# A PSUM bank for the wide Newton chains, and POOL for four groups' rotations, in a two-layer transformer kernel

## The chip, the cores and the metric

The kernel runs on one core of a Trainium2 chip. The metric is device microseconds from the start to the end of one execution; lower is better. Engines are named as in the profile: PE is the matrix engine and PEld its weight loads, DVE is VectorE, ACT is ScalarE, POOL is GpSimd, SP issues DMAs.

## The reference, cut to what matters

Two layers over x of 1024 tokens by 1024 channels. Layer 0 mixes with 12 heads of decayed causal attention, layer 1 with 12 heads of causal attention whose queries and keys come from low-rank latents; both add 4 heads of cross attention to a memory of 256 tokens. Each layer ends in a gated feed-forward with a short convolution. The change touches two things of it:

```python
def rmsnorm(x, g):
    xf = x.astype(jnp.float32)
    y = xf * lax.rsqrt(jnp.mean(xf * xf, axis=-1, keepdims=True) + EPS)
    return (y * g.astype(jnp.float32)).astype(x.dtype)

def rope(x, cos, sin):
    half = x.shape[-1] // 2
    x1, x2 = x[..., :half], x[..., half:]
    return jnp.concatenate([x1 * cos - x2 * sin, x1 * sin + x2 * cos], axis=-1)
```

Queries, keys and latents are normalised with `rmsnorm` per head; in layer 1 the last 32 of a query's 96 channels are rotated first.

## The kernel before, in words

Matmuls run in fp32r on values split in a high and a low part, so most products are three matmuls. The stages follow one another: normalisation and projection of layer 0 by six pairs of heads (`pair`, L1206), first attention (`attention`, L286), output projection (L679), feed-forward (`FFN`, L731), then projection of layer 1, second attention, output projection and feed-forward.

PSUM has three pools (L119 to L132): `psS`, two pairs of banks for scores; `psO`, one bank for attention outputs; `psX`, three banks for everything else: transposes, the chunks of the pass that finds each row's maximum, and projections. A tile takes a free buffer of its pool and gives it back after its last access.

`rsqrt` (L211) computes 1/sqrt(mean + EPS) on DVE with two setting-up instructions (L219 or L221, L222) and three Newton steps. With width 1 a step is two instructions (L228, L229). With a wider operand, 2 to 32 columns, it is three (L231 to L233). The wide form is called 21 times: six times by `pair`, twice in the memory's preparation, once for the first layer's memory queries (L1322, called before the first attention), and in layer 1 twice for its memory queries, four times by `latents` (L1590) and once by `scale_k` (L1543) of each of six groups.

A group (`Group`, L1489) is two heads of the second attention. Its pieces, in order: `begin` loads and splits the weights and sets a column of ones in the V tile (L1509); then twice: two `project`, `squares` (POOL squares, DVE sums) and `rotate`; at the end `scale_k` and `scale_q`, which multiply keys and queries by the result of `rsqrt`, on DVE and, for the rotated part of k, on POOL (L93). `rotate` calls `rope` (L1475): four multiplications and an addition and a subtraction on 128x128, two of the multiplications on POOL and the other four instructions on DVE, through a tile of the pool `tmp`, whose two buffers `squares` and the weight load share.

The order of work in the second attention: heads run one behind the other, four memory heads first. PE's order is the order of the program, since every matmul is pinned (L101 to L107, `pin`). Between the score and output units of a head, pieces of other work are put at fractions of the head's length (`TIMES`, L279; `spread`, L1674): the transposes that prepare the head after the next, the next head's maximum pass in ten chunks (matmul, then DVE, L299 or L304) and its `final` (a transpose and a DMA), and the pieces of the group two heads ahead. The order of the other engines is set by a planner at build time, from a simulated timeline (`schedule_with_timeline_sim`), by program order among what is ready in it. On POOL, the second attention also computes the low part of each block of probabilities (`plo`, L347), which the pinned output matmuls read.

The lines for the steps below: L211 to L234, L1475 to L1487, L1509, L1541, L125, L290 to L315, L522 to L526.

Of the kernel before, what the change touches and what calls it, by code (L numbers as in the profile page):

```python
# [7 lines left out]
F32 = mybir.dt.float32  # L8
# [4 lines left out]
OP = mybir.AluOpType  # L13
# [4 lines left out]
P = 128  # L18
D = 1024
S = 1024  # L20
NT = S // P
# [53 lines left out]
def hybrid_kernel(ctx: ExitStack, tc: tile.TileContext, A, out):  # L75
    nc = tc.nc
# [4 lines left out]
    def copy(eng, o, i):  # L81
        if eng == "a":
            nc.scalar.copy(o, i)  # L83
        elif eng == "v":
            nc.vector.tensor_copy(o, i)
        else:
            nc.gpsimd.tensor_copy(o, i)

    def sub(eng, o, a, b):
        (nc.vector if eng == "v" else nc.gpsimd).tensor_tensor(o, a, b, op=OP.subtract)  # L90

    def mul(eng, o, a, b):
        (nc.vector if eng == "v" else nc.gpsimd).tensor_tensor(o, a, b, op=OP.mult)  # L93

    def split(hi, lo, src, he="a", le="p"):
        copy(he, hi, src)
        sub(le, lo, src, hi.bitcast(F32))
# [27 lines left out]
    def psX():  # L125
        return psum.tile([P, 512], F32, name="psX", tag="X", bufs=3)
# [7 lines left out]
    def open_pool(name, bufs, **kw):  # L134
        return tc.alloc_tile_pool(name=name, bufs=bufs, reuse_waits="tile", **kw)

    const = open_pool("const", 1)
    small = open_pool("small", 2)
# [22 lines left out]
    ones1 = const.tile([P, 64], F32, name="ones1")  # L161
# [48 lines left out]

    def rsqrt(ss, n, width):  # L211

        v = small.tile([P, 32], F32, name="rs_v")[:, :width]
        y = small.tile([P, 32], F32, name="rs_y", bufs=6)[:, :width]
        t = small.tile([P, 32], F32, name="rs_t")[:, :width]
        if isinstance(n, tuple):
            w = width // len(n)
            for i, m in enumerate(n):
                nc.vector.tensor_scalar(v[:, i * w:(i + 1) * w], ss[:, i], 1.0 / m, EPS, op0=OP.mult, op1=OP.add)  # L219
        else:  # L220
            nc.vector.tensor_scalar(v, ss, 1.0 / n, EPS, op0=OP.mult, op1=OP.add)  # L221
        nc.vector.tensor_scalar(y.bitcast(I32), v.bitcast(I32), -0.5, 1597463007.0, op0=OP.mult, op1=OP.add)  # L222
        if width == 1:
            nc.vector.tensor_scalar(v, v, -0.5, None, op0=OP.mult)
        for i in range(3):
            if width == 1:

                nc.vector.tensor_scalar(t, y, y, v, op0=OP.mult, op1=OP.mult)  # L228
                nc.vector.tensor_scalar(y, t, 1.5, y, op0=OP.add, op1=OP.mult)  # L229
            else:  # L230
                nc.vector.tensor_tensor(t, y, y, op=OP.mult)  # L231
                nc.vector.scalar_tensor_tensor(t, t, -0.5, v, op0=OP.mult, op1=OP.mult)
                nc.vector.scalar_tensor_tensor(y, t, 1.5, y, op0=OP.add, op1=OP.mult)  # L233
        return y  # L234

# [4 lines left out]
    class Norm:  # L240
# [5 lines left out]
        def stats(self, *ts):  # L246
            ss = small.tile([P, 4], F32, name="n_ss", bufs=3)
            for i, t in enumerate(ts):
                sumsq(ss[:, i:i + 1], self.src(t), D)
            y = rsqrt(ss[:, :len(ts)], D, len(ts))  # L250
            for i, t in enumerate(ts):
                self.r[t] = y[:, i:i + 1]
# [953 lines left out]
    def pair(c, W, extra=()):  # L1206
# [4 lines left out]
        for t in range(NT):  # L1211
# [17 lines left out]
            for f in extra[:n]:  # L1229
                f()  # L1230
            del extra[:n]
        r = rsqrt(ss.rearrange("p t i -> p (t i)"), HD, 32).rearrange("p (t i) -> p t i", t=NT)
        for i, T in ((0, q), (2, k)):
            Tv = T.rearrange("p (t h d) -> p t h d", t=NT, h=2)
# [3 lines left out]
    class Memory:  # L1238
# [35 lines left out]
        def finish(self):  # L1274
            pb = [self.ps[:, t * 512:(t + 1) * 512] for t in range(2)]
            ss = small.tile([P, 2, NMH], F32, name="m_ss", bufs=1)
            for t in range(2):
                for h in range(NMH):
                    sumsq(ss[:, t, h:h + 1], pb[t][:, h * HD:(h + 1) * HD], HD)
            r = rsqrt(ss.rearrange("p t h -> p (t h)"), HD, 2 * NMH).rearrange("p (t h) -> p t h", t=2)  # L1280
            for t in range(2):
                nc.vector.tensor_tensor(kmem[:, t, :].rearrange("p (h d) -> p h d", h=NMH),
                                        pb[t][:, 0:MEM].rearrange("p (h d) -> p h d", h=NMH),
                                        r[:, t, :, None].to_broadcast([P, NMH, HD]), op=OP.mult)
                v = pb[t][:, MEM:512].rearrange("p (h d) -> p h d", h=NMH)
                copy("a", VHm[:, t, :, 0:64], v)
                sub("v", VLm[:, t], v, VHm[:, t, :, 0:64].bitcast(F32))
# [184 lines left out]
            nc.vector.tensor_scalar(r, r, 3.1415925, -3.1415925, op0=OP.min, op1=OP.max)  # L1472
            nc.scalar.activation(dst, r, AF.Sin)

    def rope(x, n, t0, nt):  # L1475

        x1, x2 = x[..., 0:16], x[..., 16:32]
        c = cos[:, t0:t0 + nt, None, :].to_broadcast([P, nt, n, 16])
        s = sin[:, t0:t0 + nt, None, :].to_broadcast([P, nt, n, 16])
        y = tmp.tile([P, 768], F32, name="rope", tag="t")[:, :4 * nt * n * 16].rearrange(  # L1480
            "p (j t n d) -> p j t n d", j=4, t=nt, n=n)
        mul("v", y[:, 0], x1, c)
        mul("p", y[:, 1], x2, s)
        mul("v", y[:, 2], x1, s)
        mul("p", y[:, 3], x2, c)
        sub("v", x1, y[:, 0], y[:, 1])
        nc.vector.tensor_tensor(x2, y[:, 2], y[:, 3], op=OP.add)  # L1487

    class Group:  # L1489

# [5 lines left out]
        def begin(self):  # L1496
            g = self.g
            raw = tmp.tile([P, 768], F32, name="g_raw", tag="t")[:, :640]
            nc.sync.dma_start(raw[:, 0:384].rearrange("p (c j) -> p c j", c=2),
                              wq[:, g * 192:(g + 1) * 192].rearrange("(c p) j -> p c j", p=P))  # L1500
            nc.sync.dma_start(raw[:, 384:640], wkv[:, g * 256:(g + 1) * 256])
            self.w = gw.tile([P, 2, 640], F32R, name="g_w")
            split(self.w[:, 0], self.w[:, 1], raw, "a", "p")
            gp, vp = gpools[g % 2], vpools[min(g % 3, 1)]
            self.q = gp.tile([P, NT, 2, QK], F32, name="gq")
            self.k = gp.tile([P, NT, 2, QK], F32, name="gk")
            self.vh = vp.tile([P, NT, 2, 65], F32R, name="g_vh")
            self.vl = vp.tile([P, NT, 2, 64], F32R, name="g_vl")
            nc.vector.tensor_copy(self.vh[:, :, :, 64], ones1[:, 0:16].rearrange("p (a b) -> p a b", a=NT))  # L1509
            self.ss = small.tile([P, 2, NT, 2], F32, name="g_ss", bufs=2)  # L1510

        def project(self, u):
# [25 lines left out]
                nc.vector.tensor_reduce(self.ss[:, j, ts], sq, axis=AX, op=OP.add)  # L1538

        def rotate(self, i):  # L1540
            rope(self.q[:, i * 4:i * 4 + 4, :, 64:96], 2, i * 4, 4)  # L1541

        def scale_k(self):  # L1543
            nc.vector.tensor_tensor(self.ss[:, 0], self.ss[:, 0], ss_kr[:, :, None].to_broadcast([P, NT, 2]), op=OP.add)
# [107 lines left out]
    def swap():  # L1652
        latent(7)
        latents(6)
        rope(kr[:, :, None, :], 1, 0, NT)
        for p in (w1, xtp, hp):
            p.release()
        pl.pf, pl.p, pl.nplo = open_pool("pf1", 2), open_pool("p1", 3), 3
        pl.pools = [open_pool("gB", 1), open_pool("vB", 2), open_pool("qkB", 1)]
        gpools.append(pl.pools[0])  # L1660
        vpools.append(pl.pools[1])
        qk_set(pl.pools[2], 1)
# [16 lines left out]
    for g in range(1, 6):  # L1679
        p = groups[g].pieces()  # L1680
# [35 lines left out]
    t0 = at[10] - 1  # L1716
    bg.setdefault(t0, []).append((0.0, turn_over))
    for j in range(6):
        i, x = divmod(t0 + 0.1 + 0.28 * j, 1.0)
# [48 lines left out]
```

## Time and profile before

| | us |
|---|---|
| median of 3 runs | 2527.79 (2522.3 to 2529.79) |
| the profiled execution | 2524.59 |
| its span, first to last instruction | 2522.8 |
| PE busy | 2369.9 (94%) |
| DVE busy | 1892.6 (75%) |
| ACT busy | 1209.5 (48%) |
| POOL busy | 985.3 (39%) |
| mean granted TensorE clock | 0.970 |

The span leaves 1.8 us of the execution outside. Busy times are unions of an engine's instructions. PE at 94% leaves some 150 us in which it waits; the views by window say where these lie.

### The profile page before, as it was taken

Reading aid. Unit: us, or ns where it says so; the run is one execution under the profiler, and the core shown is the slowest. Engines: PE = TensorE matmul, PEld = TensorE weight load, DVE = VectorE, ACT = ScalarE, POOL = GpSimd, SP = SyncE. Lnnn points to the kernel's source line nnn. Section 1 sums busy time; section 2 is a strip of 40 time slices with the busy share of each in tenths; the row PEclk is TensorE's granted clock in tenths of the full one; section 3 lists DMA queues with packets and bytes.
Section 4 is the critical chain, followed back from the end, with each engine's and each line's share of the span. In section 5 each row is a group of like instructions: output and inputs, shape, how many; then the busy total and the mean of one; then the engine's idle time right before and its main releaser. Section 6 shows DMA issues by size and latency. Waiting matters only on the chain.

```text
span 2522.8 us, 32481 instructions
## 1 busy us (share of the span) xinstructions
PE 2369.9 (94%) x11609; PEld 1954.7 (77%) x11609; DVE 1892.6 (75%) x3183; ACT 1209.5 (48%) x2341; POOL 985.3 (39%) x640
## 2 busy tenths in 40 slices
PE   7999899998999999989998798889979999998999
PEld 7999666677788888868888576767868888886887
DVE  7432677757778878789997868774488788778997
ACT  5544678723444444434454555555244444443443
POOL 1221467743233233234332566666132333233342
PEclk9999899999999999999999899989989999999999
DMA  4221121253132232451230101010512222226221
GB/s 143 84 51 27 35 61 47 52 177 109 51 92 76 84 92 76 161 190 52 99 134 11 34 23 27 19 38 22 192 56 84 87 81 84 83 85 242 84 101 67
DMA packets 163651, 208.89 MB, mean 83 GB/s; under 512 B 11175, under 2 KB 124682, under 8 KB 163490
## 3 DMA queue, kind: packets, MB, share of 16 engines
q1 hardware_dynamic: 162054, 206.63, 25.9%
q8 instruction: 92, 1.51, 0.2%
q14 instruction: 69, 0.57, 0.1%
q10 hardware_dynamic: 1436, 0.18, 0.0%
HBM read 153.34 MB, written 39.98 MB: 77 GB/s over the span
## 4 chain that ended last, share of the span: by engine, by line
PE 73%; DVE 17%; issue 3%; DMA 3%; POOL 2%; ACT 2%; SPq 0%; DVEq 0%; ACTq 0%; POOLq 0%
PE psX L102 32%; PE psS L102 25%; PE psO L102 14%; DVE f_op L90 2%; PE psX L106 2%; POOL f_op L90 1%; DVE mA L299 1%; DVE psX L304 1%; DVE f_x L1143 1%; DVE KB L525 1%; DVE f_T L90 1%; DMA rrow<-rec 1%; DVE f_d L90 1%; DVE QB L525 1%; DVE f_S L90 1%
## 5 line engine op out<-in xcount | busy, mean ns | idle before, releaser
L90 POOL TENSOR_TENSOR f_op<-f_S,f_op 128x512 fp32r<-128x512 f32 x184 | 272.0, 1479 | 671.0 <-ACT f_op L83 613.7
L102 PE MATMUL psS<-f_T,f_op 128*128 128x512 f32 x1584 | 382.4, 393 | 7.8 <-DVE f_T L90 5.9
L90 POOL TENSOR_TENSOR plo<-pf,ph 128x1024 fp32r<-128x1024 f32 (+2 forms) x160 | 315.1, 1980 | 158.0 <-ACT pf L343 95.7
L102 PEld LDWEIGHTS psS<-f_T,f_op 128*128 128x128 f32 x1584 | 297.0, 189 | 68.9 <-DVE f_T L90 6.5
L102 PE MATMUL psX<-f_B,f_op 128*128 128x512 f32 x1260 | 296.3, 389 | 0.1
L83 ACT CAST f_op<-f_S 128x512 fp32r<-128x512 f32 x248 | 153.6, 621 | 279.0 <-PE psS L102 109.2
L102 PEld LDWEIGHTS psX<-f_B,f_op 128*128 128x128 f32 x1260 | 236.4, 188 | 49.6 <-issue 0.5
L102 PE MATMUL psS<-f_op 128*128 128x512 f32 x960 | 222.4, 390 | 0.4 <-DVE f_op L90 0.4
L102 PEld LDWEIGHTS psS<-f_op 128*128 128x128 f32 x960 | 180.7, 188 | 39.0 <-DVE f_op L90 1.2
L102 PE MATMUL psX<-f_op 128*128 128x512 f32 x666 | 175.3, 403 | 20.8 <-DVE f_op L90 18.1
L102 PE MATMUL psX<-w_w,hTh 128*128 128x384 f32 (+2 forms) x672 | 167.8, 333 | 2.2 <-ACT hTh L83 2.2
L102 PEld LDWEIGHTS psX<-f_op 128*128 128x128 f32 x666 | 127.9, 194 | 54.0 <-DVE f_op L90 24.2
L898 DVE SCALAR_TENSOR_TENSOR f_v<-f_cv,cw,f_v 128x1023 f32<-128x1023 f32 x88 | 150.9, 1715 | 7.6 <-ACT f_v L896 6.2
L342 ACT ACTIVATE ph<-psS 128x1024 fp32r<-128x1024 f32 (+2 forms) x131 | 112.4, 858 | 90.4 <-PE psS L102 83.4
L83 ACT CAST f_op<-f_raw 128x512 fp32r<-128x512 f32 x148 | 91.4, 621 | 132.3 <-PE psS L102 67.1
L102 PE MATMUL psX<-KA,QA 66*128 66x128 f32 (+4 forms) x320 | 111.0, 395 | 24.5 <-DVE mA L299 10.5
L83 ACT CAST f_op<-f_d 128x512 fp32r<-128x512 f32 x144 | 84.3, 619 | 102.0 <-PE psS L102 35.6
L858 DVE TENSOR_TENSOR f_u<-psS,f_p 128x512 f32<-128x512 f32 x44 | 30.4, 691 | 126.7 <-PE psS L102 126.7
L102 PEld LDWEIGHTS psX<-w_w,hTh 128*128 128x128 f32 x672 | 120.8, 190 | 3.2 <-ACT hTh L83 2.8
L898 DVE SCALAR_TENSOR_TENSOR f_v<-f_cg,cw,f_v 128x1023 f32<-128x1023 f32 x88 | 112.6, 1279 | 11.2 <-ACT f_v L896 11.2
L90 POOL TENSOR_TENSOR f_op<-f_d,f_op 128x512 fp32r<-128x512 f32 x52 | 75.3, 1448 | 115.9 <-ACT f_op L83 115.9
L102 PE MATMUL psS<-QA,KA 67*128 67x512 f32 (+7 forms) x304 | 110.9, 366 | 7.8 <-DMA QA<-mrow 7.8
(379 smaller groups left out, 5698.8 us busy)
## 6 DMA issues: line engine op xcount, KB each, us to landing
f_raw<-in_ffn_w_up_dram SPq DMA_DIRECT2D x88, 512.0 KB
g<-f_v SPq DMA_DIRECT2D x44, 512.0 KB
f_d<-g SPq DMA_DIRECT2D x36, 512.0 KB
f_d<-in_ffn_w_down_dram SPq DMA_DIRECT2D x36, 512.0 KB
w_raw<-in_fox_w_in_dram SPq DMA_DIRECT2D x48, 192.0 KB
rrow<-rec SPq DMA_DIRECT2D x32, 256.0 KB
wo_raw<-in_w_out_dram SPq DMA_DIRECT2D x32, 256.0 KB
xr<-x SPq DMA_DIRECT2D x16, 512.0 KB
```

What stands on the lines that cost most here:

```text
L83: nc.scalar.copy(o, i)
L90: (nc.vector if eng == "v" else nc.gpsimd).tensor_tensor(o, a, b, op=OP.subtract)
L102: r = nc.tensor.matmul(*a, **k)
L106: r = nc.tensor.transpose(*a, **k)
L299: nc.vector.tensor_reduce(mA[:, q0:q0 + n], px[:, :n * width].rearrange("p (a b) -> p a b", a=n), axis=AX, op=OP.max)
L304: nc.vector.tensor_tensor_reduce(px[:, off:off + nk], px[:, off:off + nk], mQ[:, 512 - nk:], scale=1.0, scalar=m if on else NEG, op0=OP.ad ...
L342: nc.scalar.activation(ph, ps[:, :w], AF.Exp)
L525: nc.vector.scalar_tensor_tensor(Tl[tl0:tl1, hs], px, gcol, Th[0:n, hs].bitcast(F32), op0=OP.mult, op1=OP.subtract)
L858: nc.vector.tensor_tensor(o, x, y, op=OP.add)
L898: nc.vector.scalar_tensor_tensor(v[:, k:], src[:, :S - k], cw[:, 2 - k, ch:ch + 1], v[:, k:], op0=OP.mult, op1=OP.add)
L1143: nc.vector.tensor_tensor(X[t][:, hs], X[t][:, hs], self.sets[st][v], op=OP.add)
```

## The change

In `rsqrt`, calls wider than one column keep the value `v` and the temporary `t` in one tile of `psX` instead of two small SBUF tiles; the result `y` stays in SBUF. The products are regrouped so that every instruction of a step has one operand in PSUM and at most one in SBUF: t = v*y, t = -0.5*t*y, y = (t+1.5)*y. Calls of width one keep SBUF tiles, now one column wide. In the second attention, groups 2 to 5 rotate wholly on POOL and set their columns of ones there; groups 0 and 1 and the rotation of the shared key part stay as they were.

```diff
     def rsqrt(ss, n, width):
 
-        v = small.tile([P, 32], F32, name="rs_v")[:, :width]
         y = small.tile([P, 32], F32, name="rs_y", bufs=6)[:, :width]
-        t = small.tile([P, 32], F32, name="rs_t")[:, :width]
+        if width == 1:
+            v = small.tile([P, 1], F32, name="rs_v")
+            t = small.tile([P, 1], F32, name="rs_t")
+        else:
+
+            px = psX()
+            v, t = px[:, 0:width], px[:, 32:32 + width]
...
-                nc.vector.tensor_tensor(t, y, y, op=OP.mult)
-                nc.vector.scalar_tensor_tensor(t, t, -0.5, v, op0=OP.mult, op1=OP.mult)
+                nc.vector.tensor_tensor(t, v, y, op=OP.mult)
+                nc.vector.scalar_tensor_tensor(t, t, -0.5, y, op0=OP.mult, op1=OP.mult)
                 nc.vector.scalar_tensor_tensor(y, t, 1.5, y, op0=OP.add, op1=OP.mult)
...
-    def rope(x, n, t0, nt):
+    def rope(x, n, t0, nt, eng="v"):
...
-        mul("v", y[:, 0], x1, c)
+        mul(eng, y[:, 0], x1, c)
         mul("p", y[:, 1], x2, s)
-        mul("v", y[:, 2], x1, s)
+        mul(eng, y[:, 2], x1, s)
         mul("p", y[:, 3], x2, c)
-        sub("v", x1, y[:, 0], y[:, 1])
-        nc.vector.tensor_tensor(x2, y[:, 2], y[:, 3], op=OP.add)
+        sub(eng, x1, y[:, 0], y[:, 1])
+        (nc.vector if eng == "v" else nc.gpsimd).tensor_tensor(x2, y[:, 2], y[:, 3], op=OP.add)
...
-            nc.vector.tensor_copy(self.vh[:, :, :, 64], ones1[:, 0:16].rearrange("p (a b) -> p a b", a=NT))
+            copy("p" if self.g > 1 else "v", self.vh[:, :, :, 64], ones1[:, 0:16].rearrange("p (a b) -> p a b", a=NT))
...
-            rope(self.q[:, i * 4:i * 4 + 4, :, 64:96], 2, i * 4, 4)
+            rope(self.q[:, i * 4:i * 4 + 4, :, 64:96], 2, i * 4, 4, "p" if self.g > 1 else "v")
```

## Rows read from the trace of the kernel before

**Rows 1.** Windows: stretch; busy us of PE, PEld, DVE, ACT, POOL; granted clock; DMA.

```profile
110.00:270.00 160.00, 158.83 (x994) 158.00 (x992) 56.05 (x200) 74.27 (x407) 35.41 (x27) 1.00 0.15 37
...
1395.00:1460.00 65.00, 49.34 (x242) 37.77 (x243) 56.05 (x111) 31.68 (x51) 35.46 (x24) 0.82 0.14 34
...
1500.00:1532.00 32.00, 26.54 (x152) 19.59 (x151) 30.07 (x56) 17.52 (x26) 20.33 (x14) 0.95 0.14 36
1532.00:1552.00 20.00, 20.00 (x135) 16.67 (x134) 11.70 (x33) 11.59 (x21) 13.15 (x10) 1.00 0.01 1
1552.00:1584.00 32.00, 26.02 (x159) 19.40 (x158) 29.28 (x56) 18.03 (x27) 20.45 (x14) 1.00 0.14 36
...
1656.00:1700.00 44.00, 32.21 (x148) 23.27 (x147) 35.46 (x58) 20.95 (x32) 29.50 (x17) 0.77 0.20 55
```

**Rows 2.** Waits of PE from 1500 to 1700 us: total, times, longest.

```profile
PE psX L102 <- DVE mA L299: 8.3, 6, 5.5
PE psX L106 <- POOL gk L93: 7.6, 4, 3.8
PE psX L102 <- DVE KB L525: 5.9, 4, 1.5
```

**Rows 3.** DVE's groups by form, 1500 to 1700 us: busy us, mean ns | idle before.

```profile
L299 DVE TENSOR_REDUCE mA<-psX 128x1 f32<-128x512 f32 x28 | 18.6, 674 | 0.0
...
L231 DVE TENSOR_TENSOR rs_t<-rs_y 128x32 f32<-128x32 f32 x12 | 9.8, 817 | 0.0
L232 DVE SCALAR_TENSOR_TENSOR rs_t<-rs_t,rs_v 128x32 f32<-128x32 f32 x12 | 9.5, 789 | 0.0
...
L233 DVE SCALAR_TENSOR_TENSOR rs_y<-rs_t,rs_y 128x32 f32<-128x32 f32 x12 | 8.4, 698 | 0.0
...
L1509 DVE CAST g_vh<-ones 128x16 fp32r<-128x16 f32 x3 | 1.9, 643 | 0.0
```

**Rows 4.** The same view, 110 to 270 us, a step's middle instruction.

```profile
L232 DVE SCALAR_TENSOR_TENSOR rs_t<-rs_t,rs_v 128x32 f32<-128x32 f32 x15 | 2.9, 191 | 0.4
```

**Rows 5.** One line's instructions, L525, 1395 to 1765 us: ns minimum/median/maximum.

```profile
L525 DVE SCALAR_TENSOR_TENSOR QB<-psX,g_cols,QA x26: 733/737/749, 1400.4 to 1720.9; 96x512 fp32r<-96x512 f32 x24, 64x512 fp32r<-64x512 f32 x2
```

**Rows 6.** The same view of L85, 1290 to 1765 us.

```profile
L85 DVE CAST ph<-pf x13: 344/351/2220, 1414.3 to 1740.9; 128x384 fp32r<-128x384 f32 x12, 128x1024 fp32r<-128x1024 f32 x1
...
L85 DVE COPY kr<-psX x8: 173/183/193, 1304.2 to 1377.2; 128x32 f32<-128x32 f32 x8
```

**Rows 7.** Windows of the tile rope alone: its DVE and POOL instructions.

```profile
1460.00:1700.00 240.00, 15.85 (x32) 8.92 (x16) 0.94 0.11 28
```

**Rows 8.** DVE's timeline 1550 to 1582 us, group 3's chain: start, us, instruction.

```profile
1560.37 0.16 DVE L221 TENSOR_SCALAR rs_v<-g_ss 128x32 f32<-128x32 f32 x1
...
1569.17 2.28 DVE L232 SCALAR_TENSOR_TENSOR rs_t<-rs_t,rs_v 128x32 f32<-128x32 f32 x1
...
1576.36 0.17 DVE L233 SCALAR_TENSOR_TENSOR rs_y<-rs_t,rs_y 128x32 f32<-128x32 f32 x1
```

**Rows 9.** PE's timeline over the same stretch: [idle before <-releaser].

```profile
1560.49 0.44 PE L102 MATMUL psX<-KA,QA 96*128 96x384 f32 x1 [1.48 <-DVE KB L525]
...
1563.92 0.56 PE L102 MATMUL psO<-plo,g_vh 128*65 128x512 f32 x2
...
1573.54 0.27 PE L106 MATMUL psX<-ident,mA 128*8 128x128 f32 x1 [1.68 <-DVE mA L304]
...
1577.78 0.65 PE L106 MATMUL psX<-ident,gk 128*96 128x128 f32 x4 [1.25 <-POOL gk L93]
```

**Rows 10.** POOL's timeline over the same stretch.

```profile
1557.32 2.10 POOL L90 TENSOR_TENSOR plo<-pf,ph 128x896 fp32r<-128x896 f32 x1 [0.19 <-ACT pf L343]
...
1569.00 2.40 POOL L90 TENSOR_TENSOR plo<-pf,ph 128x1024 fp32r<-128x1024 f32 x1 [1.71 <-ACT pf L343]
```

**Rows 11.** DVE's timeline 1656 to 1700 us, the last group's stretch.

```profile
1675.12 2.82 DVE L90 TENSOR_TENSOR ot<-oh,ot 128x1024 fp32r<-128x1024 f32 x1
1677.87 2.32 DVE L233 SCALAR_TENSOR_TENSOR rs_y<-rs_t,rs_y 128x32 f32<-128x32 f32 x1
```

## The prediction

> **What bounds the kernel now.** The windows come first [rows 1]. In the projection of layer 0 PE is busy 158.83 of 160 us: whatever DVE or POOL saves there buys nothing. The second attention is different. From 1500 us on it alternates: stretches of 20 us in which PE is full and DVE busy 11.70, and stretches of 32 us in which PE is busy about 26 and DVE 29 to 30. Two of these stretches stand in the rows, a third between 1604 and 1636 us is like them, and the last, 1656 to 1700 us, is longer: PE 32.21 of 44. Their idle time of PE is 5.5, 6.0, some 6 and 11.8 us, 29 us together. Before that, from 1395 to 1460 us, PE idles 15.7 us.
>
> Next, who ended those waits [rows 2]: DVE, by way of psX. PE waited 8.3 us for the maximum pass to be read out, 5.9 us for a key's low part, and 7.6 us for POOL's multiplication of gk, which itself needs the end of a Newton chain. So in these stretches PE follows DVE. In group 3's, its largest waits are 1.48 us for a key's low part, 1.68 us for the end of the maximum pass and 1.25 us for gk [rows 9].
>
> Then what DVE does in them [rows 3]. Each stretch has one wide chain of 11 instructions. From 1500 to 1700 us the Newton steps are 36 instructions and take 9.8 + 9.5 + 8.4 = 27.7 us, 0.70 to 0.82 us each. The same instruction takes 191 ns where POOL is little used [rows 4]; 36 of these are 6.9 us. Some 21 us are therefore stretching, 5.2 us a chain. What stretches them is seen in two places. One step of 2.28 us starts at 1569.17 and ends at 1571.45; POOL's plo of 2.40 us runs from 1569.00 to 1571.40 [rows 8, 10]. And DVE instructions that read one operand from PSUM in these same stretches do not stretch: 26 of line 525 lie between 733 and 749 ns [rows 5], while a cast from SBUF to SBUF goes from 344 to 2220 ns [rows 6]. I read this as: an instruction of DVE that takes its operands from SBUF waits for a POOL instruction under way, and one that takes one of two from PSUM does not.
>
> **The change, part by part.**
>
> *Newton through PSUM.* Each step instruction now has one operand in PSUM, the kind that does not stretch. Gain on DVE: 5.2 us in each of the four stretches. Price of the PSUM operand: from the nearest row of the same width, a 128x32 copy out of psX at 173 to 193 ns [rows 6] against 160 ns for a narrow instruction on SBUF [rows 8], 0.02 us by 11 instructions, 0.2 us a chain. Above: the copy's longest time less 160 ns, 0.03 us, and as much again where the result goes to PSUM too, 0.06 us, 0.7 us a chain; below, nothing. I take 0.2, as the copy is the same width. [...] Of the other wide calls I cost those of `pair` and the memory at nothing: PE is full beside them, and DVE, busy 56.05 of 160 us, can't keep a bank from it for long [rows 1]. The chain that runs as the first attention begins, and those of layer 1's projection, don't stretch as a rule; their bank may cost up to 2 us together, and I take nothing.
>
> *The bank.* The chain occupies one of three psX banks from its first to its last instruction. In group 3 that is from 1560.37 to 1576.53, 16 us [rows 8], while PE sends ten chunks of the maximum pass through psX. What two banks instead of three cost isn't in the trace. Below: nothing, where DVE keeps up. Above: each of the ten chunks waits for one readout more, 0.67 us [rows 3] (8.3 us of PE's waits are already of this kind [rows 2]), 6.7 us a stretch. With the stretching gone the chain is about 10 us long and DVE has time to spare, so I take a value nearer the lower end, 1.5 us a stretch, 6 us in all.
>
> *Rotations to POOL.* From 1460 to 1700 us, 32 instructions of DVE, 15.85 us, go; 16 on POOL took 8.92 us, 0.56 us each, so POOL gains 32 x 0.56 = 17.9 us [rows 7]. That is 2.0 us of DVE for each of eight rotations. The first of a group lies where PE is full and DVE has room: nothing gained. The second lies right ahead of the chain, and PE's wait of 1.48 us follows on it, for the low part of a key queued behind [rows 9]. That wait goes. On POOL, four instructions of 0.56 us come ahead of the next plo, which moves from 1557.32 to about 1559.5, ends at 1561.6, and is read by output matmuls at 1563.92 [rows 9]: covered, by some 2 us. Were the cover gone, 2.2 us a stretch, 8.8 us. POOL still has idle time between blocks, 1.71 us before one plo [rows 10], to catch up before gk. The buffers of `tmp` are held some 2 us longer; the weight load that shares them is issued a head earlier, so nothing.
>
> *Columns of ones.* Three of 0.64 us on DVE go in this window [rows 3], half a microsecond each of the same backlog; a fourth lies in slack.
>
> *Sum.* DVE is relieved by 5.0 + 2.0 + 0.6 = 7.6 us in each of the first three stretches, more than the 6 us that PE idles there. What cannot go is the turn from chain to gk to transposes: of the 1.25 us before the transposes of gk [rows 9] I keep 1 us. So 3 x (6 - 1 - 1.5) = 10.5 us. In the last stretch DVE is also held by two splits of an attention output of 2.8 us and one more step of 2.32 [rows 11], of which only the step changes; I take 6 of 11.8 us, less 1.5 for the bank: 4.5. [...] Together 17 us; less 1 for POOL's order, 16. The start of the attention, 1395 to 1460 us, keeps its rotations, and its long chain both stretches and holds a bank: zero, plus or minus 3. The profiled execution of 2524.6 would become 2508.6; the median of the runs, 3.2 us above it, 2511.8. I give 2511.
>
> The planner orders DVE, ACT and POOL anew for the changed program. PE's order is fixed by the program, so this moves single waits; I allow 5 us either way.
>
> **The rivals.** About 0.3% (7.6 us) is what a measurement of this kernel can tell from no change.
>
> *The bank costs more than the stretching (slower).* If the planner still strews a chain's 11 instructions between the chunks for 16 us and each chunk waits, psX costs 6.7 us a stretch in four, 27 us, and as much in the two groups of the start, which get little for it, 13 us: 40 us against the 29 that DVE's relief can give at most, 2528 + 11 = 2539. It decides from about 4.8 us a chain on (29 over 6). For it: PE already waits for psX. Against: a freed DVE reads out in 0.67 us [rows 3] what PE sends every 1.3 us (ten chunks from 1560 to 1573 us [rows 9]). Chance 0.15.
>
> *No change.* PE's waits re-form: POOL, with 17.9 us more, brings gk or plo late by 2 us a stretch, and the bank takes 2 to 3 more. 2519 to 2532. For it: 7.6 us already wait for gk on POOL [rows 2]. Against: that gk waits for the chain. Chance 0.19.
>
> *All of the waits go.* If two banks do, the 29 us vanish and the clock stays up: another 5 us. 2528 - 34 = 2494. For it: in the 20 us stretches, with the same transposes and projections, PE never waits. Against: the last stretch's splits. Chance 0.11.
>
> **How the numbers follow.** The likeliest case has 0.55. Faster by over 0.3% is that case and the last, 0.66; within 0.3% 0.19; slower 0.15. The likeliest case's own range is 2502 to 2520; the unknown bank price and the other cases widen it to 2492 to 2534, which leaves out most of the slower case and the tails.
>
> **What the changed profile would show.** Right: the steps of line 231 to 233 (now with psX) at about 0.2 us from 1500 to 1700 us; no DVE instruction on the tile rope there; PE's idle time in each stretch at 2 to 3 us. Wrong by the bank: more waits of PE for psX, ended by a step of a chain. Wrong by POOL: PE's waits for gk or plo grow, with POOL busy right before. Wrong by reading: the steps still stretch, so that an operand in PSUM does not free them.

## The result, and the profile after

The changed kernel is slower: 2547.49 us (four runs, 2545.68 to 2552.92) against 2526.15 us for the kernel before, a ratio of 1.0092 [1.0073, 1.0111]. The time lies above the predicted range. The profiled execution took 2546.25 us.

The sum hides two large amounts of opposite sign. Taken from the starts of instructions on PE in the two traces:

| first or last matmul of a stage | before | after | difference |
|---|---|---|---|
| first scores of the first attention | 276.57 | 318.17 | +41.6 |
| output projection of layer 0, first | 518.43 | 554.24 | +35.8 |
| projection of layer 1, first | 1296.41 | 1333.32 | +36.9 |
| second attention, first scores | 1388.93 | 1425.24 | +36.3 |
| second attention, last output matmul | 1761.03 | 1782.32 | +21.3 |
| end | 2522.83 | 2544.35 | +21.5 |

The second attention became 15.0 us shorter (372.1 to 357.1); some 16 had been forecast. The first stage, which the prediction costed at nothing, lost 41.6 us. Some 6 us come back in the first attention, but that stretch was also 5.4 us longer in the trace of experiment 8 than before, with the same chains there, so nothing is read into it.

**The first stage.** Windows of the changed kernel over the projection of layer 0 (the row of before for 110 to 270 us is in [rows 1]), from the start to the first attention, and round one boundary between two pairs of heads; columns as in [rows 1]:

```profile
110.00:270.00 160.00, 144.92 (x803) 143.04 (x801) 46.69 (x161) 60.78 (x331) 28.23 (x21) 0.95 0.15 38
...
0.00:319.00 319.00, 271.38 (x1530) 261.98 (x1531) 137.50 (x410) 141.88 (x629) 60.60 (x53) 0.94 0.22 64
...
150.00:160.00 10.00, 10.00 (x59) 10.00 (x58) 1.68 (x5) 4.17 (x23) 1.83 (x2) 1.00 0.02 3
160.00:165.00 5.00, 1.07 (x6) 0.75 (x5) 1.84 (x6) 2.65 (x12) 1.21 (x2) 0.97 0.59 154
165.00:170.00 5.00, 5.00 (x21) 5.00 (x22) 3.61 (x12) 1.02 (x2) 2.24 (x2) 0.69 0.57 147
170.00:180.00 10.00, 10.00 (x59) 10.00 (x58) 1.47 (x6) 2.95 (x19) 1.72 (x1) 1.00 0.02 5
```

From the start to the first attention in the kernel before:

```profile
0.00:277.00 277.00, 257.68 (x1528) 250.90 (x1529) 131.00 (x397) 140.38 (x629) 56.53 (x51) 0.99 0.25 72
```

PE's idle time grew from 277 - 257.68 = 19.3 us to 319 - 271.38 = 47.6 us, by 28.3; its busy time for the same work (1528 and 1530 matmuls) grew by 13.7, while the mean granted clock fell from 0.99 to 0.94. The short windows show the two side by side: PE stands nearly still from 160 to 165 us (busy 1.07 of 5), and in the five microseconds after that the mean granted clock is 0.69: 0.50 in each of the three from 165 to 168 us, 0.95 and 1.00 in the other two. Then it is at 1.00 again. Of the other five gaps four have 2 to 6 whole microseconds at 0.50 in or behind them; at the last, before 281.88 us, the clock stays at 1.00. Who ended PE's waits from 60 to 300 us:

```profile
PE psO L102 <- ACT junk L243: 13.0, 3, 6.2
...
PE psO L102 <- DVE w_w L90: 11.3, 3, 3.9
```

Six waits, 24.3 us, one at the end of each pair (72.70, 122.94, 164.75, 203.92, 243.72 and 281.88 us). At the third, PE's timeline, then ACT's and DVE's:

```profile
164.75 0.69 PE L102 MATMUL psO<-w_w,hTh 128*128 128x384 f32 x1 [3.93 <-DVE w_w L90]
165.24 0.84 PE L102 MATMUL psX<-w_w,hTh 128*128 128x384 f32 x2
```

```profile
164.50 0.19 ACT L243 ACTIVATION_READ_ACCUMULATOR junk<-psO 128x1 f32 x1
```

```profile
164.73 0.19 DVE L226 TENSOR_SCALAR psX<-ss 128x32 f32<-128x32 f32 x1
...
168.49 0.19 DVE L238 SCALAR_TENSOR_TENSOR rs_y<-psX,rs_y 128x32 f32<-128x32 f32 x1
```

PE's next matmul goes into psO, whose one bank holds the last tile's projection until ACT has taken the last sum of squares from it, at 164.69 us. The releaser that the row names, a weight's low part at 164.72, ends at almost the same moment. What is new is that PE's next matmul is this one. The order on PE at the end of the second pair, as built, before and after (hTl7 is of the pair's last tile, hTh0 and hTh3 of the next pair's first and fourth):

```
before  MATMUL psO_1161<-w_w_795,hTl7_120 128x384
        MATMUL psX_1294<-w_w_1252,hTh0_105 128x384 x2
after   MATMUL psO_1159<-w_w_793,hTl7_120 128x384
        MATMUL psO_1479<-w_w_1248,hTh3_111 128x384 x2
```

Before, PE goes on with the next pair's first tiles, in psX. After, their psX banks are handed out behind the bank of the pair's chain. That bank's first instruction needs the same last sum, and until it is placed no later tile of psX gets a bank. Only the fourth tile, which takes psO, can be put there, and that one waits too. At the third pair's end it is the same, with one matmul of the fourth tile ahead of the first.

**The second attention.** DVE's groups from 1536 to 1722 us, the stretch of [rows 3] (line numbers from L226 on are 5 higher than before):

```profile
L93 DVE TENSOR_TENSOR oh<-oh,rrow 128x512 f32<-128x512 f32 x8 | 13.8, 1772 | 4.1 <-DMA rrow<-rec 4.1
...
L236 DVE TENSOR_TENSOR psX<-psX,rs_y 128x32 f32<-128x32 f32 x12 | 2.4, 204 | 0.1
L237 DVE SCALAR_TENSOR_TENSOR psX<-psX,rs_y 128x32 f32<-128x32 f32 x12 | 2.4, 200 | 0.3
L238 DVE SCALAR_TENSOR_TENSOR rs_y<-psX,rs_y 128x32 f32<-128x32 f32 x12 | 2.2, 184 | 0.1
```

The 36 steps take 7.0 us instead of 27.7. PE's waits in that stretch, the view of [rows 2]:

```profile
PE psX L106 <- POOL gk L93: 9.6, 3, 3.3
PE psX L106 <- DVE mA L309: 6.4, 1, 6.4
PE psX L102 <- DVE mA L309: 2.9, 1, 2.9
PE psX L102 <- DVE mA L304: 0.8, 4, 0.2
```

The wait for a key's low part (KB) is gone. Those for the maximum pass are 10.1 us, 9.3 of them two waits in the last stretch. Before they were 13.2 us and not 8.3, since [rows 2] and the prediction leave out this row of the same view:

```profile
PE psX L106 <- DVE mA L304: 4.9, 3, 1.7
```

The wait for gk has grown, from 7.6 to 9.6 us. Part of the stretching has only moved: the multiplication of oh, two SBUF operands, took 837 ns on average from 1500 to 1700 us before and takes 1772 ns now. It stands in the chain's way. In group 3 DVE, then POOL, then PE:

```profile
1604.06 3.21 DVE L93 TENSOR_TENSOR oh<-oh,rrow 128x512 f32<-128x512 f32 x2 [1.50 <-DMA rrow<-rec]
1607.19 0.18 DVE L238 SCALAR_TENSOR_TENSOR rs_y<-psX,rs_y 128x32 f32<-128x32 f32 x1
...
1604.14 2.58 POOL L90 TENSOR_TENSOR plo<-pf,ph 128x896 fp32r<-128x896 f32 x1 [0.73 <-ACT pf L348]
1608.20 2.14 POOL L93 TENSOR_TENSOR gk<-kr,rs_y 128x256 f32<-128x256 f32 x2 [1.48 <-DVE rs_y L238]
...
1609.38 1.09 PE L106 MATMUL psX<-ident,gk 128*96 128x128 f32 x4 [3.35 <-POOL gk L93]
```

DVE waits 1.50 us for a transfer, then multiplies oh for 3.21 us beside POOL's plo, and the chain's last four instructions stand behind that. POOL waits for the chain, and PE for POOL.

### The profile page after: what moved, and what is told of

Read it like the earlier page. It is cut to its first block, busy times and chain, and to the rows that moved or that the text cites. A ratio compares the mean times of both kernels' runs of the same rounds, so it can differ in the third digit from the quotient of the medians.

```text
span 2544.3 us, 32481 instructions
## 1 busy us (share of the span) xinstructions
PE 2368.9 (93%) x11609; PEld 1956.6 (77%) x11609; DVE 1868.6 (73%) x3147; ACT 1208.6 (48%) x2341; POOL 1001.3 (39%) x676
## 4 chain that ended last, share of the span: by engine, by line
PE 57%; DVE 11%; issue 2%; DMA 1%; ACT 1%; POOL 1%; SPq 0%; DVEq 0%; POOLq 0%; ACTq 0%
PE psX L102 24%; PE psS L102 22%; PE psO L102 10%; DVE f_op L90 2%; PE psX L106 1%; DVE f_x L1148 1%; POOL f_op L90 1%; DVE f_S L90 1%; DVE f_d L90 1%; DVE f_T L90 1%; DVE oh L93 0%; DVE f_S L1091 0%; DMA rrow<-rec 0%; DVE f_v L903 0%; DVE f_B L90 0%
## 5 line engine op out<-in xcount | busy, mean ns | idle before, releaser
L102 PE MATMUL psX<-w_w,hTl 128*128 128x384 f32 (+2 forms) x336 | 114.5, 341 | 1.6 <-DVE hTl L90 1.6
```

Source lines behind the costliest of these rows:

```text
L102: r = nc.tensor.matmul(*a, **k)
```

## Experiments: where the loss comes from

My theory after the comparison: the loss is the place of the chain's request for a psX bank in the program's text, ahead of the next pair's tiles. Rivals: the time for which the chain holds the bank, and a higher price of operands in PSUM.

**1. Chains in PSUM only from layer 1 on**, all else as changed.

```diff
-        else:
+        elif in_psum[0]:
             px = psX()
             v, t = px[:, 0:width], px[:, 32:32 + width]
+        else:
+            v = small.tile([P, 32], F32, name="rs_v32")[:, :width]
+            t = small.tile([P, 32], F32, name="rs_t32")[:, :width]
...
+    in_psum[0] = True
     l1 = open_pool("l1", 1)
```

> The changed kernel, but the wide chains of layer 0 (pairs, memory, memory queries) keep value and temporary in SBUF; layer 1 is as changed. Theory (claim): psX banks are handed out in program order, and a pair's chain claims one ahead of the next pair's tiles though it can only start when the last tile's sums are done; so layer 0 returns to the kernel before (first scores of the first attention at 277 us instead of 318) and the second attention keeps its 357 us from first scores to last output matmul (372 before): 2526 - 15 = about 2511. Rival (whole-kernel replanning): the gain in the second attention depends on the shifted start, and layer 0 loses by another order: 2520 to 2535.

Measured: 2511.74 us against 2523.23, ratio 0.9953 [0.9936, 0.9971]. The first attention starts at 276.94 us, 0.4 later than before; the second takes 360.0 us, 12.1 less. So all of the loss lies in layer 0's chains and all of the gain in layer 1.

**2. Only the request**: the kernel before, with the chain in SBUF as it was, and ahead of each pair's chain a copy of its sums into a psX tile that nothing reads.

```diff
+        nc.vector.tensor_copy(psX()[:, 0:32], ss.rearrange("p t i -> p (t i)"))
         r = rsqrt(ss.rearrange("p t i -> p (t i)"), HD, 32)...
```

> The kernel before, all chains in SBUF, no work on POOL moved; only, ahead of each of the six pairs' chains, one DVE copy of the sums into a psX tile that nobody reads. Claim theory: the copy holds its bank for 0.2 us but claims it ahead of the next pair's tiles, so PE idles 3 to 6 us at each of six pair boundaries as in the changed kernel, first scores at 300 to 318 us, 2550 to 2562 us in all. Rival (hold): a bank held for 0.2 us instead of 2 to 4 costs next to nothing, 2526 to 2531. Rival (price of operands in PSUM): no chain reads PSUM, so 2526.

Measured: 2557.52 us in one run. The first attention starts at 314.88 us, 38.3 later than before, with six gaps of 22.4 us together. PE's waits from 60 to 300 us:

```profile
PE psO L102 <- ACT junk L238: 11.5, 3, 4.5
PE psO L102 <- DVE w_w L90: 10.9, 3, 3.7
```

And the copy on DVE's timeline:

```profile
161.54 0.19 DVE L1232 COPY psX<-ss 128x32 f32<-128x32 f32 x1
```

It holds the bank for 0.19 us instead of the chain's 4 (164.73 to 168.68 us above), and no Newton step touches PSUM, yet the loss is nearly whole. Both rivals fall.

**3. Another pool**: the changed kernel with layer 0's chains in psS, which the projection of tiles doesn't use.

```diff
-            px = psX()
+            px = psS() if in_S[0] else psX()
```

> The changed kernel, but layer 0's wide chains take their PSUM tile from psS, which is little used while layer 0 projects, instead of psX. Claim theory: no claim on psX, so no idle time of PE at the pair boundaries, first scores at 277 to 282 us, about 2511 to 2516 in all. Rival (price of operands in PSUM): the chains still read PSUM, so the loss of layer 0 stays, first scores near 318, 2547.

Measured: 2512.34 us in one run. The boundary gaps are gone, and the first attention starts 4.2 us later than before. The chain is in PSUM as in the changed kernel, with the same 11 instructions in its bank; only nothing queues behind it.

**4. The same request later in the text**: the pair's chain, still in psX, comes behind the next pair's third tile.

```diff
             pb = project(W, t)
+            if t == 2 and held:
+                held.pop()()
...
-        r = rsqrt(ss.rearrange("p t i -> p (t i)"), HD, 32)...
+        def scale():
+            r = rsqrt(ss.rearrange("p t i -> p (t i)"), HD, 32)...
+        held.append(scale)
```

> The changed kernel, but each pair's chain and the scaling behind it are traced after the third tile of the next pair (the last pair's after the third tile of the memory queries); still in psX. Claim theory: the claim stands behind the tiles that it blocked, so the 3 to 6 us of idle time at six boundaries go; the memory queries' chain, right ahead of the first attention, still claims psX first, so first scores at 280 to 295 us, 2513 to 2525 in all. Rival (hold): the chain still occupies one of three banks for 2 to 4 us while PE projects, only a little later, so the idle times move and stay, 2540 to 2550.

Measured: 2533.71 us in one run, 9 above the range that I had given; the first attention starts at 290.52 us, 13.9 later than before instead of 41.6. One boundary gap is left, 3.9 us at 114.97 us, at the end of the pair beside which the memory's preparation asks for its own bank, and that request I had not moved:

```profile
PE psO L102 <- ACT junk L243: 3.9, 1, 3.9
```

The other five are gone. The place in the text decides about them. What the rest of the 13.9 us consists of was not taken apart.

## Experiments: where the gain comes from

**5. The chains alone**: the six groups' chains in psX, every other chain in SBUF, rotations and columns of ones on DVE as before.

```diff
-    def rsqrt(ss, n, width):
+    def rsqrt(ss, n, width, psum=False):
...
-        else:
+        elif psum:
...
-            rope(self.q[:, i * 4:i * 4 + 4, :, 64:96], 2, i * 4, 4, "p" if self.g > 1 else "v")
+            rope(self.q[:, i * 4:i * 4 + 4, :, 64:96], 2, i * 4, 4)
```

> The kernel before, with value and temporary in psX for the six groups' chains of the second attention alone; rotations and columns of ones stay on DVE. First scores of the second attention to its last output matmul take 372.1 us before, 357.1 as changed, 360.0 with all of the change in layer 1 alone. Theory (the stretching of the steps is most of what PE waits for): chain steps at 0.2 us, 362 to 366 us, 2514 to 2519 in all. Rival (the rotations ahead of the chain are most of it): 368 to 371 us, 2520 to 2524. Rival (the bank eats the gain): 372 or more, 2524 to 2530.

Measured: 2523.62 against 2523.35 us, ratio 0.9997 [0.9987, 1.0007]. The steps take 192, 208 and 184 ns, yet the second attention takes 369.3 us, 2.9 less than before, and my expectation for it is missed. The number is the one that the first rival gave (the rotations are most of it); experiment 6 tests that. PE's waits from 1500 to 1700 us:

```profile
PE psX L106 <- POOL gk L93: 11.0, 4, 3.7
PE psX L102 <- DVE KB L533: 5.9, 4, 1.5
PE psX L102 <- DVE mA L307: 4.6, 6, 3.1
```

The waits for the maximum pass fell from 13.2 to 4.6 us, but the wait for KB is as it was [rows 2], and the wait for gk took 3.4 us more. 20 us less on DVE alone bought nothing that can be measured.

**6. The rotations alone**: the changed kernel with every chain in SBUF (the edit of experiment 1, never switched on).

> The changed kernel with every chain in SBUF: only the rotations and columns of ones of groups 2 to 5 on POOL. Theory: each of the four stretches loses the 1.5 us wait behind the rotation and 0.5 us more, the steps of the chain still stretch (0.7 to 0.8 us each): 364 to 368 us of second attention, 2517 to 2521 in all. Rival (POOL becomes late): plo or gk come later, 372 to 380 us, 2524 to 2532.

Measured: 2539.82 us against 2523.35, ratio 1.0060 [1.0045, 1.0076]: slower than before by 16 us. The second attention takes 386.7 us, outside what I and the rival had expected. PE's waits from 1500 to 1716 us:

```profile
PE psS L102 <- DMA QA<-mrow: 20.3, 4, 5.9
PE psX L102 <- DVE KB L535: 7.0, 4, 1.8
```

DVE's timeline ahead of the longest of them:

```profile
1636.60 1.70 DVE L93 TENSOR_TENSOR oh<-oh,rrow 128x512 f32<-128x512 f32 x2
1638.23 3.60 DVE L93 TENSOR_TENSOR gk<-gk,rs_y 128x512 f32<-128x512 f32 x2
1641.75 2.61 DVE L93 TENSOR_TENSOR gq<-gq,rs_y 128x768 f32<-128x768 f32 x2
1644.28 0.27 DVE L322 TENSOR_SCALAR mrow<-psX 8x128 fp32r<-8x128 f32 x1
```

`mrow` is the row of negated maxima (`final`); the next head's scores wait for its transfer. Before, in group 3, it stood ahead of the multiplication of gk; here the planner put it behind 7.9 us of multiplications. And the wait for KB, which the prediction took away by the rotations, is still there.

**7. The old grouping of the products**: the kernel of experiment 5 with the value in SBUF again and t = y*y, so that one instruction in three has two SBUF operands.

```diff
-                nc.vector.tensor_tensor(t, v, y, op=OP.mult)
-                nc.vector.scalar_tensor_tensor(t, t, -0.5, y, op0=OP.mult, op1=OP.mult)
+                nc.vector.tensor_tensor(t, y, y, op=OP.mult)
+                nc.vector.scalar_tensor_tensor(t, t, -0.5, v, op0=OP.mult, op1=OP.mult)
```

> As the chain alone in the groups, but with the old grouping of the products: the temporary in psX, the value in SBUF, so that the first instruction of a step squares y, with both its operands in SBUF, and the other two have one operand in each. Theory (an instruction with both operands in SBUF waits for POOL, one with an operand in PSUM does not): only the squaring stretches, to 0.7 to 0.9 us a piece from 1500 to 1700 us, the other two stay at 0.2 us. Rival (any instruction that reads SBUF stretches, or what stretches is the write of the temporary): all three stay at 0.2 us, or all three stretch.

Measured: 2521.70 us in one run. DVE's groups by form, 1500 to 1700 us:

```profile
L239 DVE TENSOR_TENSOR psX<-rs_y 128x32 f32<-128x32 f32 x12 | 9.4, 780 | 0.0
L240 DVE SCALAR_TENSOR_TENSOR psX<-psX,rs_v 128x32 f32<-128x32 f32 x12 | 2.4, 200 | 0.0
L241 DVE SCALAR_TENSOR_TENSOR rs_y<-psX,rs_y 128x32 f32<-128x32 f32 x12 | 2.1, 178 | 0.1
```

The one with both inputs in SBUF stretches, the two beside it, with one input in PSUM, do not. The prediction's reading of what stretches a step is shown for these.

**8. Groups' chains and rotations together**, every other chain in SBUF.

> Only the six groups' chains of the second attention use a psX bank; rotations and columns of ones on POOL as in the changed kernel; every other wide chain is in SBUF. Theory (all of the gain lies in the groups' chains and the rotations together, all of the loss in the claim of layer 0): first scores of attention 0 within 1 us of before, the second attention 357 to 361 us instead of 372, the time 11 to 14 us under the kernel before, the ratio 0.994 to 0.996. Rival (the chains of layer 1's projection and of the memory matter as well, and the run that used PSUM from layer 1 on gained part of its 12 us there): only 4 to 8 us under the kernel before.

Measured: 2511.54 against 2524.24 us, ratio 0.9945 [0.9924, 0.9965]; the first attention starts 0.1 us later than before, the second takes 359.4 us. So the groups' chains and the rotations hold the whole gain, and the chains of layer 1's projection add nothing. The parts don't add up: nothing for the chains, 16 us lost for the rotations, 13 us gained together.

**9. The same with the chain first**: the groups' chains given a priority 200 instructions earlier, because PE still waited for gk.

```diff
-            self.r = rsqrt(..., QK, 32)...
+            with tc.high_priority(offset=200):
+                self.r = rsqrt(..., QK, 32)...
```

> psX only for the six groups' chains, rotations on POOL, layer 0 and the rest of layer 1 with chains in SBUF, and the chain of a group given to the planner with the priority of 200 instructions earlier. In the changed kernel PE still waits 3.0 to 3.4 us in three groups for the transposes of gk, whose chain stands on DVE behind a 3 us multiplication by the softmax sums. Theory (that place in DVE's order sets the wait): these waits go, second attention 350 to 354 us, 2503 to 2508 in all. Rival (gk waits for POOL, which multiplies kr and follows its own queue): the waits stay near 3 us, 357 to 360 us, 2510 to 2514.

Measured: 2514.66 against 2523.35 us, ratio 0.9965 [0.9946, 0.9984]. The waits for gk stay:

```profile
PE psX L106 <- POOL gk L93: 8.1, 3, 3.5
```

This tests nothing. The planner built the same program as in experiment 8, instruction by instruction on every engine, so the 3 us between the two are the scatter between two series of runs. My theory, that the chain's place among DVE's other work sets this wait, stays open, and the rows speak for it. In group 2 of this trace oh starts between two of POOL's blocks:

```profile
1524.46 1.29 DVE L93 TENSOR_TENSOR oh<-oh,rrow 128x512 f32<-128x512 f32 x2 [0.82 <-DMA rrow<-rec]
...
1528.80 0.64 PE L106 MATMUL psX<-ident,gk 128*96 128x128 f32 x4 [1.68 <-POOL gk L93]
```

There oh takes 1.29 us and PE waits 1.68 for gk; in group 3 oh takes 2.80 us and PE waits 3.49. In groups 2 to 4 of experiment 11 it is 1.29, 2.09 and 1.29 us of oh, and waits of 1.74, 3.43 and 1.73. That is a connection and not a test: no run with the chains in PSUM put all of the chain ahead of oh.

**10 to 12. The row of maxima on ACT.** Since experiment 6 lost its time through `mrow`, these move its one instruction in layer 1 from DVE to ACT: in the kernel of experiment 6 (10), in that of 8 (11) and in the kernel before (12).

```diff
-                nc.vector.tensor_scalar(row, px[:8, :P], -1.0, None, op0=OP.mult)
+                if on_act[0]:
+                    nc.scalar.activation(row, px[:8, :P], AF.Identity, scale=-1.0)
+                else:
+                    nc.vector.tensor_scalar(row, px[:8, :P], -1.0, None, op0=OP.mult)
```

> The rotations alone (all chains in SBUF), and in layer 1 the row mrow is written by ACT instead of DVE, so that it no longer stands behind the multiplications of oh, gk and gq. Theory (the 15 us that the rotations alone lost are mrow's place on DVE): PE's waits for mrow, 20.3 us in four, fall to under 4 us; the second attention takes 366 to 374 us instead of 386.7, the time is 2519 to 2528. Rival (the stretched chain itself makes DVE late, and mrow was only the first to be waited for): another wait takes its place, KB or gk, at 4 us or more each, the second attention stays over 380 us and the time over 2534.

> The kernel with the groups' chains in a psX bank and the rotations on POOL, and mrow on ACT as well. Theory (what is left of PE's waits there is gk's turn on POOL and the splits of the last stretch, neither of which mrow delays): within 3 us of the kernel without mrow's move, 2508 to 2514. Rival (DVE is still what is late): 4 us or more under it, with the waits for gk shorter by 0.5 us each.

> The kernel before with one edit: in layer 1 the row mrow is written by ACT instead of DVE. Theory (mrow's place on DVE costs by itself, and the change is not needed for that gain): PE's waits of 5.5 us for mrow's transfer and 4.3 us for mrow's bank in the second attention go, the time is 5 to 10 us under the kernel before, 2514 to 2519. Rival (before the change the stretched chains set the pace, and the move pays only once they are short): within 4 us of the kernel before, with PE's waits moved to KB or gk.

Experiment 10: 2521.77 us in one run, 18 us under experiment 6; the second attention takes 366.7 us. The wait for `mrow` is gone. The one for KB stays, and one for gq, smaller than that for `mrow`, is new (1500 to 1716 us):

```profile
PE psX L102 <- DVE KB L540: 7.1, 4, 1.8
PE psX L106 <- DVE gq L93: 6.5, 3, 2.7
...
PE psS L102 <- DMA QA<-mrow: 0.3, 1, 0.3
```

Experiment 11: 2501.23 us (2493.18 to 2505.25) against 2524.24, ratio 0.9904 [0.9881, 0.9928]: the fastest of all, 10 us under experiment 8. I had expected no effect; the rival, that DVE was still late, holds. The windows of the second attention, experiment 8, then experiment 11. Its profiled run was its fastest (2493.18 us) and that of experiment 8 among its slowest (2514.83), so the two windows differ by more than the medians do:

```profile
1393.00:1752.00 359.00, 316.22 (x1840) 247.65 (x1839) 244.43 (x513) 203.82 (x311) 239.72 (x182) 0.91 0.11 27
```

```profile
1387.00:1732.00 345.00, 309.65 (x1843) 242.98 (x1842) 238.56 (x498) 206.18 (x326) 242.13 (x182) 0.94 0.11 29
```

PE's idle time falls from 42.8 to 35.4 us, and its busy time by 6.6, with the mean granted clock at 0.94 instead of 0.91. The waits for gk from 1500 to 1716 us fall from 9.6 us to this:

```profile
PE psX L106 <- POOL gk L93: 6.9, 3, 3.4
```

Experiment 12: 2524.17 against 2520.70 us, ratio 1.0017 [1.0006, 1.0029], as the rival had it. In the second attention the waits for `mrow` fell from 10.1 to 2.8 us, but those for KB grew from 8.0 to 12.6 us. So the same move gives nothing in the kernel before, 18 us where the rotations are on POOL and the chains stretch (10 against 6), and 10 us where the chains are in PSUM too (11 against 8). It pays behind the rotations on POOL, whether the chains stretch or not; with the chains in PSUM and the rotations on DVE it was not run.

## Why the prediction was wrong

**The step that failed** is this sentence: "Of the other wide calls I cost those of `pair` and the memory at nothing: PE is full beside them, and DVE, busy 56.05 of 160 us, can't keep a bank from it for long [rows 1]." I priced the bank by how long it is held. The cost is in where it is asked for: the chain's first instruction needs the pair's last sum, and all psX tiles behind it in the text stood behind that. Six gaps of 24.3 us and 13.7 us more of busy time at the lower clock (0.94 against 0.99) are 38 of the 41.6 us; a hold of 0.19 us in experiment 2 costs nearly the same. That PE was full [rows 1] was a sign that the stage could only lose.

A second sentence fell with it: "PE's order is fixed by the program, so this moves single waits; I allow 5 us either way." PE's order is fixed so in the second attention, where the matmuls are pinned, and even there the new order of DVE cost 15 us in experiment 6. In layer 0 the order on PE was built anew, and the allowance was too small by a factor of eight.

**The rival that came true in sign** was the bank's cost, but not as I told it. I placed it in the second attention, as chunks waiting while the chain holds its bank, and gave as its sign "more waits of PE for psX, ended by a step of a chain". It came in layer 0, as waits for psO ended by ACT's last sum. Its price of 6.7 us a stretch in the second attention shows in no run: the chain in psX ends no wait of PE there of more than 0.23 us. What two banks instead of three cost inside the waits for the maximum pass, 13.2 us before and 10.1 after, no run takes apart.

**Newton through PSUM**: right. The 36 steps went from 27.7 to 7.0 us, 20.7 where 4 times 5.2 was forecast. The price of the PSUM operand, taken at 0.2 us a chain, is under 0.1 (199 ns against 191 for a step's middle instruction, below). The second half of the mechanism, which I did not have, is that POOL's blocks stay and stretch another instruction of DVE beside them: oh, from 837 to 1772 ns. It stands ahead of the chain's end, so PE waits longer for gk. POOL was not busy right before gk, as my sign for that rival had it; it stood idle for 1.48 us until the chain ended.

**Rotations**: the term was mis-attributed. The KB wait does go, but neither the rotations nor the chains take it away alone (7.0 us in experiment 6, 5.9 in 5). That the rotations by themselves would cost 16 us, most of it through `mrow`'s place on DVE (experiment 10 takes 18 us back), no step of mine held.

**The sum of the second attention**, 16 us forecast and 15.0 measured, came out right by terms that were not. The windows of the whole second attention, before:

```profile
1389.00:1761.00 372.00, 323.06 (x1841) 250.23 (x1841) 268.86 (x548) 204.81 (x311) 232.02 (x147) 0.93 0.10 27
```

And after:

```profile
1425.00:1782.00 357.00, 314.25 (x1841) 246.11 (x1840) 244.28 (x513) 204.06 (x312) 245.66 (x182) 0.92 0.11 28
```

PE's idle time fell only from 48.9 to 42.8 us, by 6.2. In the four stretches it fell from 29 to 20, by 9 where 15 had been forecast, and at the start it grew by some 3. I kept 1 us before each transposition of gk; 3.2 stayed (9.6 in three). In the last stretch 4.5 us of 11.8 were to go, and the two waits for the maximum pass alone are 9.3. The sum had the two splits of 2.8 us there; ahead of the last chunk's readout DVE also has a split of a weight, 2.34 us, and this:

```profile
1709.48 4.22 DVE L93 TENSOR_TENSOR oh<-oh,rrow 128x512 f32<-128x512 f32 x2
```

The other 8.8 us are busy time of PE for the same 1841 matmuls. The sum reckoned with 2 us for the granted clock, and the last rival with 5; no run shows such a term by itself. Here the mean granted clock did not rise (0.93 and 0.92), so what shortened the busy time stays open.

## What to carry to other kernels

Before a temporary is put into a pool that others share, look at where its request stands in the text, and at what its first instruction needs: a request that comes due late can hold up all requests behind it, however short its life (0.19 us of hold in experiment 2, and the next stage 38.3 us later), here in a stage where the bounding engine was full (PE busy 158.83 of 160 us [rows 1]). Give it a pool that nothing behind it uses, or put it behind the next tiles. Change one engine's load and look at the whole order that the planner builds: of three edits here each alone gave nothing or a loss, and together 1.0%. An edit that leaves this order as it was, as in experiment 9, tests nothing.

## What the hardware showed that I had not expected

A 128x32 step with an operand in PSUM is hardly slower than one with all operands in SBUF. From 110 to 290 us, where nothing stretched it before [rows 4], the same step takes

```profile
L237 DVE SCALAR_TENSOR_TENSOR psX<-psX,rs_y 128x32 f32<-128x32 f32 x15 | 3.0, 199 | 0.4
```

199 ns against 191. The setting-up instruction whose only input is in PSUM (L227) takes 191 ns there against 181 before (L222).

The stretching is not limited to instructions with two SBUF inputs. In experiment 6 the chain's first instruction, with one input, took 1.99 us where it takes 0.16 before [rows 8] (before, one of the six took 1.50 as well):

```profile
1620.33 1.99 DVE L231 TENSOR_SCALAR rs_v<-g_ss 128x32 f32<-128x32 f32 x1
```

POOL's plo runs beside it:

```profile
1620.20 2.09 POOL L90 TENSOR_TENSOR plo<-pf,ph 128x896 fp32r<-128x896 f32 x1
```

It ends at 1622.29, and DVE's at 1622.32. Experiment 7 shows the stretching for an instruction with two SBUF inputs (780 ns, against 200 and 178 for those with one in PSUM); this row shows a TENSOR_SCALAR with one SBUF input held up as well.
